# Six pairs of input-projection column tiles by Strassen's seven products

## The chip, the cores and the metric

The kernel runs on one core of one Trainium2 chip. The metric is the device time of one execution, in microseconds (us); a time given for a kernel is the median of its runs. The engines are TensorE (PE), VectorE (DVE), ScalarE (ACT), GpSimd (POOL) and SyncE (SP, which here only issues DMAs).

## The reference

Two layers, each a mixer with a residual and then a cross-attention with a residual; a last RMSNorm. All in float32, sequence 1024, model width 1024. The part that matters here is the mixer's input projection: one matrix product, whose 3200 output columns (25 tiles of 128) feed three groups of heads.

```python
xn = rms_norm(h, norm_mix[l])
proj = xn @ w_in                     # (1024 x 1024) @ (1024 x 3200)
gq, gk, gv, glr, ggate, cc, cb, ch, cgate, cq, ckv, kr, mgate = split(proj)
o_gla  = rms_norm(gla_chunked(gq, gk, gv, log_a(glr)), gla_norm) * silu(ggate)
o_conv = cb * causal_conv3(cc * ch, conv_w) * silu(cgate)
qh, kvh = rms_norm(cq, g) @ w_uq, rms_norm(ckv, g) @ w_ukv
o_mla  = causal_attention(rope(qh), rope(kvh, kr)) * silu(mgate)
h = h + concat(o_gla, o_conv, o_mla) @ w_out
```

## The kernel before, in words

**Products.** Activations lie transposed: 128 features on the partitions, 512 positions in a row, so the model width is eight tiles k, and the sequence two halves c. PE multiplies in a reduced type, so each operand is a sum of a high and a low part (`_h`, `_l`), and `mm3` (L298) makes a product of three matmuls: hi·hi (L301), hi·lo (L302), lo·hi (L303), each 128x512.

**The input projection** (`win`, L393). A column tile i of `w_in` is loaded by SP as 128x1024 (`wraw`, L118, two buffers "wr"), ACT casts the high part (L127), and the low part is subtracted in two halves of 128x512 by POOL, or for every fourth tile by DVE (`wsplit`, L123; `sub`, L149). Then for each half c 8 x 3 = 24 matmuls sum into one PSUM bank, and DVE multiplies the bank by R, the reciprocal norm of each position (L402). The gain of the norm is already in the split activations `x1` (`h_x_h`, `h_x_l`). A layer has 25 tiles: 0 to 6 GLA's q, k, v; 7 to 9 its gate `gg`; 10 to 13 and 14 to 17 the convolution's `cc`, `ch`, `cb`, `cg` for two blocks; 18, 19 the latent `cq`; 20, 21 the latent `ckv`; 22 to 24 the attention's gate `mg`. Each gate tile goes through `silu` (L405): three ACT operations, one on DVE, one on ACT, and a product on POOL.

**GLA** has a front (`gla_front`, one chain per pair of heads, over ACT, POOL and DVE), transposes of the values (`v_tokens`, L442: PE transposes `gvt`, ACT copies them out at L453), and a body (`gla_body`, L526) of many small matmuls (`at`, `o`, `up`, `kTps`), whose POOL share is `osq` (128x384).

**What sets the order.** `layers` (L1143 to L1199) takes generators and weaves them: a yield is a piece of work, and `weave` and `chain` say which piece is written when. From that program order a scheduler makes a fixed order of instructions for each engine. Each engine runs its list in order; a semaphore wait holds up all that stands behind it on that engine. Tiles come from pools with a fixed number of buffers (`BUFS`). SP has one list for all DMAs.

In the stretch at stake each layer writes gates and the first convolution block as fill between the pieces of the two GLA bodies, then the two latents (`latent`, L670), each with its own two column tiles, then the second convolution block (`conv`, L626), with the rotary key `krope` and the first keys `mla_k` between, then the attention.

Of the kernel before, what the change touches and what calls it, by code (L numbers as in the profile page):

```python
# [22 lines left out]
KT = D // P  # L23
# [32 lines left out]
def chain(*gens):  # L56
    for g in gens:
        yield from g


def run(g):
    for _ in g:
        pass


BUFS = {"s": 64, "p": 9, "pt": 4, "tq": 1}
# [14 lines left out]
    "wk": (0, 2), "wv": (0, 2), "wq": (0, 2),  # L81
}


class Trunk:
# [344 lines left out]

    def in_q(self, l, p, tags=("mm", "S")):
        self.gq[p] = self.g2(f"gq{l}_{p}")
        yield from self.win(l, 5 * p, f"gq{l}_{p}", lambda c: self.gq[p][c], tags)
# [71 lines left out]
    def gla_start(self, l):  # L505
# [16 lines left out]
        for c in range(2):  # L522
            for dst, (q, r) in enumerate(((0, 64), (1, 0), (1, 0), (0, 64))):
                nc.sync.dma_start(self.kr[c][dst * 16 : dst * 16 + 16], self.gq[q][c][r : r + 16])
# [101 lines left out]
    def conv(self, l, j):  # L626
        nc = self.nc
        base = 10 + 4 * j
        tags = PAIR[f"conv{j}"]
        u = self.g2(f"cc{l}_{j}")  # L630
        y = self.g2(f"cy{l}_{j}")
        self.cy[j] = y
        yield from self.win(l, base, f"cc{l}_{j}", lambda c: u[c], tags)
        tmp = {}

        def dst(name):
            def f(c):
                tmp[c] = self.g(f"{name}{l}_{j}_{c}", tag="pt")
                return tmp[c]
            return f  # L640

        w = [self.gain(l, "conv", 2 * k + j) for k in range(3)]
        c = 0
        for _ in self.win(l, base + 1, f"ch{l}_{j}", dst("ch"), tags):
            self.mul(nc.gpsimd, u[c], u[c], tmp[c])
            nc.scalar.activation(y[c], u[c], AF.Copy, scale=w[2])
            for s in (1, 2):
                nc.vector.scalar_tensor_tensor(
                    y[c][:, s:], u[c][:, : 512 - s], w[2 - s], y[c][:, s:], op0=ALU.mult, op1=ALU.add
                )  # L650
                if c == 1:
                    nc.vector.scalar_tensor_tensor(
                        y[1][:, :s], u[0][:, 512 - s :], w[2 - s], y[1][:, :s], op0=ALU.mult, op1=ALU.add
                    )
            c += 1
            yield
        c = 0
        for _ in self.win(l, base + 3, f"cg{l}_{j}", dst("cg"), tags):
            self.silu(tmp[c], f"cgs{l}_{j}_{c}")
            self.mul(nc.gpsimd, y[c], y[c], tmp[c])  # L660
            c += 1
            yield
        c = 0
        for _ in self.win(l, base + 2, f"cb{l}_{j}", dst("cb"), tags):
            self.mul(nc.gpsimd, y[c], y[c], tmp[c])
            c += 1
            yield


    def latent(self, l, what, base):  # L670

        nc = self.nc
        raw = [self.g2(f"{what}{l}_{i}") for i in range(2)]
        acc = self.g2(f"{what}acc{l}", tag="pt")
        for i in range(2):
            c = 0
            for _ in self.win(l, base + i, f"{what}{l}_{i}", lambda c: raw[i][c], PAIR[f"lat{i}"]):
# [6 lines left out]
                c += 1  # L684
                yield
# [446 lines left out]
    def go(self, out):  # L1132
        tc = self.tc
        self.mgd = [self.dram(f"mgd{i}_", 2, [P, 512]) for i in range(3)]
        self.ggd = [self.dram(f"ggd{i}_", 2, [P, 512]) for i in range(3)]
        self.god = self.dram("god", NT, [P, 384])
# [6 lines left out]
    def layers(self, out):  # L1143
        for l in range(self.depth):
# [11 lines left out]
            run(self.in_q(l, 1, PAIR["q1"]))  # L1156
            if l == 0:
                run(self.mem_prelude())
            run(self.in_k(l, 1, PAIR["k1"]))
            if l == 0:  # L1160
                self.rope_args()
            self.gla_start(l)
            gates = [self.gate(l, 22 + i, self.mgd[i], f"mg{l}_{i}") for i in range(3)]
            values = chain(*(self.in_v(l, f, PAIR["gv"]) for f in (1, 2)), gates[0])
            weave((values, 0.75), (chain(self.gla_front(l, 0), self.gla_front(l, 1)), 1))
            vt = self.v_tokens(l)
            next(vt)
            next(gates[1])
            run(vt)
            fill = chain(  # L1170
                *gates[1:],
                *(self.gate(l, 7 + i, self.ggd[i], f"gg{l}_{i}") for i in range(3)),
                self.conv(l, 0),
            )
            bodies = [self.gla_body(l, 0), self.gla_body(l, 1)]
            for _ in range(4):
                for b in bodies:
                    next(b, None)
                    for _ in range(2):
                        next(fill, None)  # L1180
            for b in bodies:
                run(b)
            run(fill)
# [4 lines left out]
            conv = self.conv(l, 1)  # L1188
            run(self.latent(l, "ckv", 20))
            run(self.latent(l, "cq", 18))  # L1190
            self.wkn = self.mla_w(l, 2)
            for _ in range(2):
                next(conv)
            run(self.krope(l))
            run(self.mla_k(l, 0))
            run(conv)
# [224 lines left out]
```

## Time and profile before

| what | before |
|---|---|
| median of 3 runs (lowest to highest) | 1416.45 us (1416.19 to 1418.07) |
| the profiled execution: its time, its span | 1415.69 us, 1413.9 us |
| PE busy | 1382.9 us (98%) |
| DVE, ACT, POOL busy | 771.0 (55%), 690.0 (49%), 571.7 us (40%) |
| DMA moved | 131.13 MB, 93 GB/s over the span |
| granted TensorE clock over the span | 0.997 |

The span is what the engines' records cover; the execution's time is 1.8 us more. Busy time is the union of an engine's instructions. Matmuls are pipelined, so that the duration of one (0.39 us) is longer than the distance from one to the next.

### The profile page before, as it was taken

To read this page: it belongs to the slowest core of one execution; us is meant where nothing else is said; L and a number is where in the kernel's file an instruction comes from. 1 tells how busy PE (TensorE), PEld (TensorE's weight loads), DVE (VectorE), ACT (ScalarE), POOL (GpSimd) and SP (SyncE) were. 2 spreads that over 40 slices of the span, in tenths; PEclk is the share of its full clock that TensorE was granted. 3 is DMA by queue.
4 is the path that set the end of the run, shared out by engine and by line. 5 is a ranking of instruction groups with operands and counts; after the bars stand their busy time and mean duration, and the time that the engine had idled before them with its cause. 6 is when DMAs were issued, how large, how long until landed. Compare 5 with 4: busy or idle time off the path is not lost.

```text
span 1413.9 us, 19744 instructions
## 1 busy us (share of the span) xinstructions
PE 1382.9 (98%) x7132; PEld 1128.0 (80%) x7132; DVE 771.0 (55%) x1431; ACT 690.0 (49%) x1462; POOL 571.7 (40%) x584
## 2 busy tenths in 40 slices
PE   7998999999999999999999999999999999999998
PEld 6787888888776688888878788888887767888886
DVE  7846445364788554545653632534657883553533
ACT  5446544253777442555431653424557773344543
POOL 6325335215556452353342532441356663414320
PEclk9999999999999999999999999999999999999999
DMA  8131222122122254321522121211232123534403
GB/s 310 53 129 53 77 76 74 47 63 91 45 61 65 92 172 134 121 89 46 185 100 82 49 78 53 89 58 45 83 86 60 33 81 112 194 105 142 156 1 120
DMA packets 61827, 131.13 MB, mean 93 GB/s; under 512 B 7553, under 2 KB 14497, under 8 KB 61729
## 3 DMA queue, kind: packets, MB, share of 16 engines
q1 hardware_dynamic: 61728, 129.87, 28.5%
q8 instruction: 56, 0.92, 0.3%
q14 instruction: 43, 0.34, 0.1%
HBM read 95.76 MB, written 33.55 MB: 91 GB/s over the span
## 4 chain that ended last, share of the span: by engine, by line
PE 83%; DVE 9%; ACT 3%; issue 2%; DMA 2%; POOL 1%; SPq 0%; DVEq 0%; POOLq 0%; ACTq 0%
PE op_ps L301 4%; PE op_ps L302 4%; PE op_ps L303 4%; PE av L848 4%; PE pt L834 3%; PE xqps L301 2%; PE xqps L302 2%; PE xqps L303 2%; PE s L301 2%; PE gg_ps L301 2%; PE gg_ps L303 2%; PE gg_ps L302 2%; PE s L303 1%; PE s L302 1%; DVE gla_a L479 1%
## 5 line engine op out<-in xcount | busy, mean ns | idle before, releaser
L149 POOL TENSOR_TENSOR win_l<-win_r,win_h 128x512 fp32r<-128x512 f32 x76 | 104.1, 1391 | 196.4 <-ACT win_h L127 191.6
L805 POOL TENSOR_SCALAR p<-p,sm 128x128 f32<-128x128 f32 (+3 forms) x144 | 87.8, 619 | 63.8 <-DVE sm L803 41.5
L127 ACT CAST win_h<-win_r 128x1024 fp32r<-128x1024 f32 x50 | 52.4, 1049 | 123.5 <-PE gg_ps L302 36.6
L303 PE MATMUL op_ps<-mix_h,wout_l 128*128 128x512 f32 x256 | 99.9, 390 | 0.0
L302 PE MATMUL op_ps<-mix_l,wout_h 128*128 128x512 f32 x256 | 99.8, 390 | 0.0
L301 PE MATMUL op_ps<-mix_h,wout_h 128*128 128x512 f32 x256 | 99.0, 393 | 0.0
L799 ACT ACTIVATE p<-s,nm 128x128 f32<-128x128 f32 (+3 forms) x144 | 83.2, 581 | 27.1 <-DVE nm L795 13.8
L791 DVE TENSOR_REDUCE nm<-s 128x1 f32<-128x128 f32 (+3 forms) x144 | 78.4, 551 | 3.1 <-PE s L303 1.1
L834 PE MATMUL pt<-ident,p 128*128 128x128 f32 x432 | 70.6, 280 | 1.6 <-POOL p L805 1.5
L834 PEld LDWEIGHTS pt<-ident,p 128*128 128x128 f32 x432 | 49.7, 140 | 27.3 <-issue 13.7
L848 PE MATMUL av<-ph,V 128*64 128x256 f32 x480 | 69.6, 375 | 0.0
L149 POOL TENSOR_TENSOR wout_l<-wout_r,wout_h 128x512 fp32r<-128x512 f32 x32 | 43.3, 1376 | 42.5 <-ACT wout_h L127 34.4
L301 PE MATMUL s<-k_h,q_h 128*128 128x128 f32 (+3 forms) x144 | 55.2, 386 | 1.3 <-ACT p L799 0.6
L301 PEld LDWEIGHTS op_ps<-mix_h,wout_h 128*128 128x128 f32 x256 | 47.7, 188 | 10.5 <-issue 0.8
L302 PEld LDWEIGHTS op_ps<-mix_l,wout_h 128*128 128x128 f32 x256 | 48.1, 188 | 9.9
L303 PEld LDWEIGHTS op_ps<-mix_h,wout_l 128*128 128x128 f32 x256 | 48.1, 188 | 9.8
L842 ACT COPY ph<-pt 128x512 f32<-128x512 f32 (+1 forms) x72 | 39.6, 549 | 23.7 <-PE pt L834 20.6
L301 PE MATMUL xqps<-op_x_h,wq_h 128*128 128x512 f32 x128 | 51.1, 399 | 0.0
L1005 POOL TENSOR_SCALAR xp<-xp,xsm 128x256 f32<-128x256 f32 x64 | 29.8, 482 | 51.4 <-DVE xsm L1003 51.3
L303 PE MATMUL xqps<-op_x_h,wq_l 128*128 128x512 f32 x128 | 50.4, 393 | 0.0
L302 PE MATMUL xqps<-op_x_l,wq_h 128*128 128x512 f32 x128 | 50.2, 392 | 0.0
L302 PE MATMUL s<-k_l,q_h 128*128 128x128 f32 (+3 forms) x144 | 49.9, 347 | 0.0
(502 smaller groups left out, 4292.5 us busy)
## 6 DMA issues: line engine op xcount, KB each, us to landing
win_r<-in_w_in SPq DMA_DIRECT2D x50, 512.0 KB, 3.6
wout_r<-in_w_out SPq DMA_DIRECT2D x16, 512.0 KB, 4.0
x<-in_x SPq DMA_DIRECT2D x16, 256.0 KB, 6.3
hd<-h SPq DMA_DIRECT2D x16, 256.0 KB, 4.0
op0r<-hd SPq DMA_DIRECT2D x16, 256.0 KB, 4.0
hd<-op0r SPq DMA_DIRECT2D x16, 256.0 KB, 2.9
wq_r<-in_w_mem SPq DMA_DIRECT2D x8, 512.0 KB, 3.8
wk_r<-in_w_mem SPq DMA_DIRECT2D x8, 512.0 KB, 3.6
```

Of the source, the lines that this page charges most:

```text
L127: ins = self.nc.scalar.copy(hi, raw)
L149: eng.tensor_tensor(lo, src, hi.bitcast(F32), op=ALU.subtract)
L301: nc.tensor.matmul(ps, a[0], b[0], start=first, stop=False, **k)
L302: nc.tensor.matmul(ps, a[0], b[1], start=False, stop=False, **k)
L303: nc.tensor.matmul(ps, a[1], b[0], start=False, stop=last, **k)
L791: nc.vector.tensor_reduce(nm[:, b : b + 1], ps[:, :w], axis=AX.X, op=ALU.max, negate=True)
L799: nc.scalar.activation(x[:, :w], ps[:, :w], AF.Exp, bias=nm[:, 0:1], accum_out=sm[:, b : b + 1])
L805: nc.gpsimd.tensor_scalar(pr[b][:, :w], pr[b][:, :w], sm[:, 0:1], 1.0, op0=ALU.mult, op1=ALU.mult)
L834: nc.tensor.transpose(ps[:, o : o + P], prob[qi][kt // 4][:, (kt % 4) * P : (kt % 4 + 1) * P], self.ident,)
L842: nc.scalar.copy(pt[:, :w], ps[:, :w])
L848: nc.tensor.matmul(av[own if j == 0 else other, q0:256], self.V[kt][:, 64 * h : 64 * h + 64], pt[:, j * 256 : j * 256 + 256 - q0], start=( ...
L1005: nc.gpsimd.tensor_scalar(pr[:, j], pr[:, j], sm[:, j : j + 1], 1.0, op0=ALU.mult, op1=ALU.mult)
```

## The change

Per layer 12 of the 25 column tiles are taken in six pairs, `PAIRS` = (20, 21), (18, 19), (10, 11), (13, 12), (14, 15), (17, 16). For a pair, the product is a 2 x 2 block product: the halves of the model width (k 0 to 3, k 4 to 7) by the two tiles on one side, the two halves of the sequence on the other. It is computed with seven block products of 4 x 3 = 12 matmuls (Winograd's form) in place of eight. For this:

- `a_side` loads the layer's input `hd` again (16 loads of 128x512), ACT puts the gain on (16), POOL multiplies by R (16) and makes the four sums of the activations (16), SP stores them (16, `sd`). `s_parts` loads the sums back (16), ACT casts the high parts, and DVE (k 0, 2) or POOL (k 1, 3) subtracts the low ones.
- `w_first` makes, per pair, the split weights of the first tile (`wsplit`), two sums of the second by the first in place (two POOL subtractions of 128x512), a further sum `t4` on DVE, its cast on ACT and its low part on DVE, and stores the sums (512 KB, `wtd`). `w_second`, twice per pair, loads 768 KB or 512 KB of weights and sums, makes a further sum the first time (POOL or DVE), casts on ACT, and subtracts low parts, half on POOL, half on DVE.
- `wave1` runs three block products per pair and stores two of them (`pd`), `wave2` two and stores two partial sums (`ud`), `wave3` the last two. DVE takes each out of PSUM, with R or with a stored sum, and POOL adds once. The results go to sinks, from which `conv` and `latent` take them; their own projections are gone.
- In `layers` value tile 1 stands before the memory prelude, the first GLA front is written among values and q, the transposes of the values stand before the second front, and `rope_args` (layer 0) after it. The gates still fill the first pieces of the GLA bodies, with `a_side` beside them, and wave 1 and `s_parts` come after the gates. Waves 2 and 3 run for the latents' pairs first, and for the four pairs of the convolution in and after the latents.
- "wr" has 4 buffers in place of 2, "s" 60 in place of 64.

```diff
-BUFS = {"s": 64, "p": 9, "pt": 4, "tq": 1}
+BUFS = {"s": 60, "p": 9, "pt": 4, "tq": 1}
+PAIRS = ((20, 21), (18, 19), (10, 11), (13, 12), (14, 15), (17, 16))
-        raw = self.wp.tile(shape, F32, tag="wr", bufs=2, name=name + "_r")
+        raw = self.wp.tile(shape, F32, tag="wr", bufs=4, name=name + "_r")
+    def a_side(self, l):
+        for k in range(4):
+            t = {}
+            for m, c in ((k, 1), (k + 4, 1), (k, 0), (k + 4, 0)):
+                x = self.g(f"sa{l}_{m}_{c}")
+                nc.sync.dma_start(x, self.hd[m][c])
+                nc.scalar.activation(x, x, AF.Copy, scale=self.gain(l, "mix", m))
+                self.mul(nc.gpsimd, x, x, self.R[c])
+                t[(m // 4, c)] = x
+            a11, a12, a21, a22 = t[(0, 0)], t[(1, 0)], t[(0, 1)], t[(1, 1)]
+            nc.gpsimd.tensor_tensor(a22, a21, a22, op=ALU.add)
+            nc.gpsimd.tensor_tensor(a21, a11, a21, op=ALU.subtract)
+            nc.gpsimd.tensor_tensor(a11, a22, a11, op=ALU.subtract)
+            nc.gpsimd.tensor_tensor(a12, a12, a11, op=ALU.subtract)
+            for j, x in enumerate((a22, a11, a21, a12)):
+                nc.sync.dma_start(self.sd[j][k], x)
+            yield
+    def w_first(self, l, n):
...
+        r1, r2 = raws
+        hi, lo = self.wsplit(r1, sh, f"win{l}_{i1}")
+        nc.gpsimd.tensor_tensor(r2[:, :4], r2[:, :4], r1[:, :4], op=ALU.subtract)
+        nc.gpsimd.tensor_tensor(r2[:, 4:], r2[:, 4:], r2[:, :4], op=ALU.subtract)
+        t4 = self.g(f"t4_{l}_{n}", tag="tq", shape=[P, 4, P])
+        nc.vector.tensor_tensor(t4, r1[:, 4:], r2[:, 4:], op=ALU.subtract)
+        nc.sync.dma_start(self.wtd[n], r2)
+        nc.scalar.copy(w4[:, :4], t4)
+        self.sub(nc.vector, w4[:, 4:], t4, w4[:, :4])
...
+    def w_second(self, l, n, j):
...
+        if j == 0:
+            nc.sync.dma_start(r, src)
+            (nc.vector if n % 2 else nc.gpsimd).tensor_tensor(r[:, 4:], r[:, 4:], r[:, :4], op=ALU.subtract)
+            nc.sync.dma_start(r[:, :4], self.wtd[n][:, 4:])
+        else:
+            nc.sync.dma_start(r[:, :4], self.wtd[n][:, :4])
+            nc.sync.dma_start(r[:, 4:], src[:, 4:])
+        nc.scalar.copy(hi, r)
+        for h, e in ((0, nc.gpsimd), (4, nc.vector)):
+            self.sub(e, lo[:, h : h + 4], r[:, h : h + 4], hi[:, h : h + 4])
...
+    def wave2(self, l, pairs):
...
+        for n in pairs:
+            if n != pairs[-1]:
+                head(n + 1)
+                yield
+            p4 = self.spilled(l, f"q4_{l}_{n}", self.pd[n][1])
+            self.prod(x[n], w[n][1], s3, False)
+            u = self.g(f"u3_{l}_{n}", tag="pt")
+            nc.vector.tensor_tensor(u, x[n], p1[n], op=ALU.add)
+            nc.sync.dma_start(self.ud[n][1], u)
+            k = self.sink[PAIRS[n][0]]
+            nc.gpsimd.tensor_tensor(k.tile(1), u, p4, op=ALU.add)
+    def wave3(self, l, pairs):
...
+            u3 = self.spilled(l, f"v3_{l}_{n}", self.ud[n][1])
+            self.prod(y[n], w[n][0], s1, True)
+            k = self.sink[PAIRS[n][1]]
+            nc.vector.tensor_tensor(k.tile(1), y[n], u3, op=ALU.add)
...
     def layers(self, out):
...
+            sides = self.a_side(l)
+            first = self.wave1(l)
+            parts = chain(self.s_parts(l, 1), self.s_parts(l, 2))
+            for i in range(7):
+                next(bodies[(i + 1) % 2], None)
+                next(sides, None)
+                if i > 2:
+                    next(parts, None)
+                    next(parts, None)
+                for _ in range(2):
+                    if next(fill, 0) == 0:
+                        next(first, None)
+                        next(first, None)
...
+            weave((self.wave2(l, (0, 1)), 1), (chain(self.s_parts(l, 0), self.s_parts(l, 3)), 2))
+            run(self.wave3(l, (0, 1)))
+            rest = self.wave2(l, (2, 3, 4, 5))
```

Counted over the two layers, PE has 4364 matmuls of 128x512 in place of 4508, POOL 420 two-input operations of 128x512 in place of 286, DVE 472 in place of 378, SP 734 DMAs in place of 466 (244 more of 256 KB and 24 more of 512 KB).

Three places of the order, layer 0. **POOL, up to the weights of tile 17.** Before, this is the step from the latents to the second convolution block (`_l` tiles are low parts that PE reads):

```order
L149 TENSOR_TENSOR win_18_l<-win_18_r,win_18_h 128x512 x2
L149 TENSOR_TENSOR wlat_2_l<-wlat_2_r,wlat_2_h 128x384 x2
L149 TENSOR_TENSOR win_14_l<-win_14_r,win_14_h 128x512 x2
L149 TENSOR_TENSOR win_17_l<-win_17_r,win_17_h 128x512 x2
L152 TENSOR_TENSOR cc_1_0_2546<-cc_1_0_2546,ch_1_0_2703 128x512
```

In the change it is the end of wave 1 (`win_16_r` and the like are weight sums, `sl` low parts of activation sums, `w2r` a sum for wave 2):

```order
L519 TENSOR_TENSOR win_12_r<-win_12_r 128x512
L518 TENSOR_TENSOR win_15_r<-win_15_r,win_14_r 128x512
L183 TENSOR_TENSOR win_13_l<-win_13_r,win_13_h 128x512 x2
L183 TENSOR_TENSOR sl_2_1_2160<-sr_2_1_2157,sh_2_1_2159 128x512
L519 TENSOR_TENSOR win_15_r<-win_15_r 128x512
L518 TENSOR_TENSOR win_16_r<-win_16_r,win_17_r 128x512
L519 TENSOR_TENSOR win_16_r<-win_16_r 128x512
L183 TENSOR_TENSOR win_14_l<-win_14_r,win_14_h 128x512 x2
L183 TENSOR_TENSOR sl_2_3_2303<-sr_2_3_2300,sh_2_3_2302 128x512
L186 TENSOR_TENSOR osq_1_7_2284<-osb_1_6_2262 128x384
L537 TENSOR_TENSOR w2r_0_0_2513<-w2r_0_0_2513 128x512
L183 TENSOR_TENSOR win_17_l<-win_17_r,win_17_h 128x512 x2
```

What stood nearly alone among waits for ACT is now the tail of a list of POOL work that begins with `a_side`.

**PE, at the first use of tile 17's low part.** Before:

```order
L706 MATMUL yps_1_2622<-krp_1_2623,dup 128x512
L301 MATMUL cg_1_ps_2749<-h_x_h_197,win_17_h 128x512
L302 MATMUL cg_1_ps_2749<-h_x_l_198,win_17_h 128x512
L303 MATMUL cg_1_ps_2749<-h_x_h_197,win_17_l 128x512
L301 MATMUL cg_1_ps_2749<-h_x_h_210,win_17_h 128x512
```

and in the change (`wx_5`, `wy_5` are the banks of the last pair in wave 1):

```order
L337 MATMUL wy_4_2392<-h_x_h_457,w_0_4_2351 128x512
L335 MATMUL wx_5_2454<-h_x_h_247,win_17_h 128x512
L336 MATMUL wx_5_2454<-h_x_l_248,win_17_h 128x512
L335 MATMUL wy_5_2455<-h_x_h_433,w_0_5_2422 128x512
L336 MATMUL wy_5_2455<-h_x_l_434,w_0_5_2422 128x512
L337 MATMUL wx_5_2454<-h_x_h_247,win_17_l 128x512
L335 MATMUL wx_5_2454<-h_x_h_260,win_17_h 128x512
```

It comes over 300 rows earlier on PE (row 1018 in place of row 1325), right behind the GLA bodies and the gates.

**SP, behind the rotary key.** Before, the key's two halves are stored (`yd`) and read back (`k`), with weight loads among them:

```order
L712 DMA yd_0_92<-yh_0_2615 128x512
L712 DMA yd_0_94<-yl_0_2616 128x512
L120 DMA wlat_0_r<-in_w_lat 128x768
L751 DMA k_0_h_2633<-yd_0_92 64x512
L751 DMA k_1_h_2637<-yd_0_92 64x512
```

In the change the partial sums of the last two pairs (`ud`, from DVE) are stored behind the key's stores, and the sum `v_0_4` is read back from what was just stored:

```order
L920 DMA yd_1_143<-yh_1_3010 128x512
L920 DMA yd_1_145<-yl_1_3011 128x512
L608 DMA ud_1_125<-u_0_4_3030 128x512
L608 DMA ud_1_127<-u_0_5_3049 128x512
L580 DMA v_0_4_3137<-ud_1_125 128x512
L580 DMA v_0_3_3176<-ud_0_122 128x512
L874 DMA cgl_0_0_3204<-cgd_0_84 128x512
```

A round trip through memory that had no counterpart now stands in SP's list between wave 2 and wave 3.

## Rows read from the trace of the kernel before

**Rows 1.** The page, its first part: busy time and share of each engine.

```profile
PE 1382.9 (98%) x7132; PEld 1128.0 (80%) x7132; DVE 771.0 (55%) x1431; ACT 690.0 (49%) x1462; POOL 571.7 (40%) x584
```

**Rows 2.** The page, chain of work that ended last: shares by engine.

```profile
PE 83%; DVE 9%; ACT 3%; issue 2%; DMA 2%; POOL 1%; SPq 0%; DVEq 0%; POOLq 0%; ACTq 0%
```

**Rows 3.** PE's waits: engine, line, for whom: us in total, times, longest.

```profile
PE gvt L449 <- ACT gv L453: 7.1, 3, 4.5
```

**Rows 4.** Timeline of PE: start, us, line, tiles, count, idle before and releaser.

```profile
127.42 1.28 PE L449 MATMUL gvt<-ident,vf 128*128 128x128 f32 x6 [4.46 <-ACT gv L453]
...
128.93 0.63 PE L302 MATMUL mg_ps<-h_x_l,win_h 128*128 128x512 f32 x1
129.35 0.63 PE L303 MATMUL mg_ps<-h_x_h,win_l 128*128 128x512 f32 x1
```

**Rows 5.** Timeline of PE in the stretch of the GLA bodies.

```profile
205.79 0.39 PE L303 MATMUL ch_ps<-h_x_h,win_l 128*128 128x512 f32 x1
...
215.11 0.39 PE L302 MATMUL ch_ps<-h_x_l,win_h 128*128 128x512 f32 x1
...
216.25 0.60 PE L545 MATMUL at<-gq,gk 128*128 128x128 f32 x4
216.69 0.49 PE L569 MATMUL up<-gv,kT 128*128 128x192 f32 x2
217.01 0.61 PE L545 MATMUL at<-gq,gk 128*128 128x128 f32 x4
...
219.31 0.35 PE L558 MATMUL o<-gv,atb 128*128 128x96 f32 x2
...
220.11 0.48 PE L303 MATMUL ch_ps<-h_x_h,win_l 128*128 128x512 f32 x1
```

**Rows 6.** Windows: stretch, length, busy of PE, PEld, DVE, ACT, POOL, PEclk, DMA share, GB/s.

```profile
13.00:40.00 27.00, 26.20 (x125) 21.24 (x125) 25.66 (x28) 15.63 (x27) 23.45 (x16) 1.00 0.79 284
...
129.00:135.00 6.00, 6.00 (x28) 4.99 (x27) 0.69 (x1) 2.74 (x6) 2.11 (x2) 0.82 0.37 142
99.00:345.00 246.00, 240.81 (x1170) 202.52 (x1169) 119.62 (x183) 112.62 (x207) 93.45 (x78) 0.99 0.20 65
```

**Rows 7.** Window 0 to 13 us, same columns.

```profile
0.00:13.00 13.00, 5.92 (x19) 3.27 (x19) 5.75 (x12) 4.41 (x6) 2.76 (x8) 1.00 0.78 252
```

**Rows 8.** Groups of POOL between 99 and 345 us, by shape: busy, mean ns, idle before.

```profile
L152 POOL TENSOR_TENSOR osq<-osb 128x384 f32<-128x384 f32 x8 | 6.6, 826 | 10.7 <-ACT osb L579 10.7
...
L152 POOL TENSOR_TENSOR cy<-cy,cg 128x512 f32<-128x512 f32 x4 | 5.2, 1291 | 0.3
```

**Rows 9.** Groups of DVE between 99 and 345 us, by shape.

```profile
L149 DVE TENSOR_TENSOR win_l<-win_r,win_h 128x512 fp32r<-128x512 f32 x8 | 5.4, 720 | 0.5 <-ACT win_h L127 0.3
```

**Rows 10.** Timelines of POOL and of DVE, 26 to 32 us.

```profile
26.19 4.70 POOL L292 TENSOR_TENSOR h_acc<-h_acc,h_sq 128x512 f32<-128x512 f32 x3
...
26.23 1.80 DVE L163 SCALAR_TENSOR_TENSOR h_x_l<-h,gains,h_x_h 128x512 fp32r<-128x512 f32 x1
27.95 0.68 DVE L351 COPY h<-xt 128x512 f32<-128x512 f32 x1
28.56 1.18 DVE L163 SCALAR_TENSOR_TENSOR h_x_l<-h,gains,h_x_h 128x512 fp32r<-128x512 f32 x1
...
30.26 1.17 DVE L163 SCALAR_TENSOR_TENSOR h_x_l<-h,gains,h_x_h 128x512 fp32r<-128x512 f32 x1
```

**Rows 11.** Timelines of DVE and POOL, the gate tile's second half.

```profile
153.56 0.69 DVE L402 TENSOR_TENSOR mg<-mg_ps,h_acc 128x512 f32<-128x512 f32 x1 [0.46 <-PE mg_ps L303]
...
158.73 1.29 POOL L152 TENSOR_TENSOR mg<-mg,mg_2s 128x512 f32<-128x512 f32 x1
```

**Rows 12.** DMA issues: queue, count, KB each, median us from issue to landing.

```profile
op0r<-hd SPq DMA_DIRECT2D x16, 256.0 KB, 4.0
...
mgd<-mg SPq DMA_DIRECT2D x12, 256.0 KB, 2.0
```

**Rows 13.** The page, costliest groups: busy, mean ns of one, idle before.

```profile
L127 ACT CAST win_h<-win_r 128x1024 fp32r<-128x1024 f32 x50 | 52.4, 1049 | 123.5 <-PE gg_ps L302 36.6
```

More of the change, by code (lines that the diff above doesn't have):

```diff
@@ new lines, in s_parts, with prod @@
+    def s_parts(self, l, j):
+        nc = self.nc
+        self.Sp[j] = []
+        for k in range(4):
+            raw = self.g(f"sr{l}_{j}_{k}", tag="pt")
+            nc.sync.dma_start(raw, self.sd[j][k])
+            hi, lo = self.g(f"sh{l}_{j}_{k}", F32R), self.g(f"sl{l}_{j}_{k}", F32R)
+            self.split(hi, lo, raw, eng=self.pick("sp", k))
+            self.Sp[j].append((hi, lo))
+            yield
+    def prod(self, ps, w, xs, first):
+        for k, x in enumerate(xs):
+            self.mm3(ps, w(k), x, first and k == 0, k == len(xs) - 1, skip_group_check=True)
@@ new lines, in wave3, with head @@
+    def wave3(self, l, pairs):
+        nc = self.nc
+        s1, s4 = self.Sp[0], self.Sp[3]
+        w, y = {}, {}
+        def head(n):
+            w[n] = self.w_second(l, n, 1)
+            y[n] = self.psum(("S", "mm", "S", "t")[n % 4], f"vy{l}_{n}")
+            u3 = self.spilled(l, f"v3_{l}_{n}", self.ud[n][1])
+            self.prod(y[n], w[n][0], s1, True)
+            k = self.sink[PAIRS[n][1]]
+            nc.vector.tensor_tensor(k.tile(1), y[n], u3, op=ALU.add)
+        head(pairs[0])
+        yield
+        for n in pairs:
+            if n != pairs[-1]:
+                head(n + 1)
+                yield
+            u2 = self.spilled(l, f"v2_{l}_{n}", self.ud[n][0])
+            self.prod(y[n], w[n][1], s4, False)
+            k = self.sink[PAIRS[n][1]]
+            nc.vector.tensor_tensor(k.tile(0), y[n], u2, op=ALU.add)
+            k.done(0)
+            k.done(1)
+            yield
+            if n in self.after:
+                yield from self.after[n]
@@ L431, in in_q, with sinks @@
+    def sinks(self, l):
+        self.sink = {}
+        for j in range(2):
+            self.sink[13 + 4 * j] = GateSink(self, self.cgd[j], f"cg{l}_{j}")
+            for i in range(3):
+                self.sink[10 + 4 * j + i] = Sink(self, f"c{i}{l}_{j}")
+        for i in range(18, 22):
+            self.sink[i] = Sink(self, f"lat{l}_{i}")
     def in_q(self, l, p, tags=("mm", "S")):
@@ L672, in latent @@
         nc = self.nc
[L673 to L674 removed]
+        raw = [self.sink[base + i].t for i in range(2)]
+        acc = self.g2(f"{what}acc{l}", tag="p")
         for i in range(2):
[L676 to L677 removed]
+            for c in range(2):
                 if i == 0:
@@ L1155, in layers @@
             weave(*((g, 1) for g in head))
-            run(self.in_q(l, 1, PAIR["q1"]))
+            run(self.in_v(l, 1, PAIR["gv"]))
             if l == 0:
                 run(self.mem_prelude())
-            run(self.in_k(l, 1, PAIR["k1"]))
+            self.gla_start(l)
+            fill = chain(self.in_v(l, 2, PAIR["gv"]), self.in_q(l, 1, PAIR["q1"]))
+            weave((fill, 1), (self.gla_front(l, 0), 1))
+            for c in range(2):
+                self.kr_rows(l, c, 1)
+            vt = self.v_tokens(l)
@@ new lines, in layers @@
+            k1 = self.in_k(l, 1, PAIR["k1"])
+            next(vt)
+            next(k1)
+            run(vt)
+            run(k1)
+            gates = [self.gate(l, 22 + i, self.mgd[i], f"mg{l}_{i}") for i in range(3)]
+            gates += [self.gate(l, 7 + i, self.ggd[i], f"gg{l}_{i}") for i in range(3)]
+            bodies = [self.gla_body(l, 0), self.gla_body(l, 1)]
+            fill = chain(*gates)
+            front = self.gla_front(l, 1)
+            for i in range(4):
+                next(front)
+                next(fill)
+                if i == 1:
+                    next(bodies[0])
@@ L1160, in layers @@
+            run(front)
             if l == 0:
                 self.rope_args()
[L1162 to L1180, printed above, removed]
+            self.sinks(l)
+            self.Sp = [None] * 4
+            sides = self.a_side(l)
[11 more added lines that the diff above has]
+                        next(first, None)
@@ L1181, in layers @@
             for b in bodies:
                 run(b)
-            run(fill)
+            run(sides)
+            weave((first, 1), (parts, 1))
             if l == 0:
```

158 lines of the change are left out of this document (119 added, 39 removed).

## The prediction, made before the kernel ran

> **What bounds the kernel now.** I first read the shares of the engines [rows 1]: PE is busy 98% of the span, the next engine, DVE, 55%, POOL 40%. The chain of work that ended last says the same of the path: 83% of it is PE [rows 2]. So time taken from PE is time of the kernel, as long as no other engine is made late for it, and what has to be read is the room that the others have in the one stretch that the change rewrites. That is 99 to 345 us in layer 0, and its twin in layer 1. There PE is busy 240.8 of 246 us, DVE 119.6, ACT 112.6, POOL 93.5, and the DMA engines 20% [rows 6]. Averages leave room for much; the order of the lists decides.
>
> The price of one matmul of 128x512 is not its 0.39 us, which overlaps its neighbours. From the start at 205.79 to the start at 215.11 us there are 41 steps [rows 5], so 9.32 / 41 = 0.227 us each.
>
> **What the change removes.** PE loses 144 matmuls: 144 x 0.227 = **-32.7 us**. Nothing hides this part, since PE is on the path wherever they stood.
>
> A second gain is a by-product. PE waits 7.1 us for ACT's copies of the transposed values, 4.5 of them at once [rows 3], and the matmuls behind that wait stand 0.42 us apart at first [rows 4]; over 129 to 135 us the granted clock is 0.82 [rows 6], so the first part of it ran at the lower of the clock's two levels, after an idle PE. In the changed list of ACT the copies stand before the second GLA front instead of behind it, with 44 matmuls (10 us) on PE between the first front's last step and the first transposes. The bounds are 0 and 7.1 us plus 0.18 x 6 = 1.1 us of slow clock; since the first front's chain is still ahead, I take a little over half: **-5 us**.
>
> **What it adds on POOL.** 134 operations of 128x512, half per layer, at 1.29 us [rows 8]: 67 x 1.29 = 86 us on top of 93.5 in a stretch that becomes some 230 us long. On average they fit. But they stand in one run. From the product of the last `mg` half to the low part of tile 17 (first place of the order) I count 59 operations of 128x512 and 7 of 128x384: 59 x 1.29 + 7 x 0.83 = 81.9 us. The run can't start before that half's silu is ready for POOL, 158.73 - 153.56 = 5.2 us after DVE begins to take it out of PSUM [rows 11]. So POOL's list needs 87.1 us. PE comes to that low part after 316 matmuls (71.7 us) and 98 small GLA matmuls: each float32 matmul has two records there, so two `at` take 216.69 - 216.25 = 0.44 us, one `up` 0.32, four `o` 220.11 - 219.31 = 0.80 [rows 5]. With 34 at 0.22 (`at` and `kTps`), 12 at 0.32 and 52 at 0.20, that is 21.7 us, 93.4 in all. POOL would be 6.3 us early if nothing disturbed it.
>
> Two things do. The first is DVE. POOL's three sums at 26.19 us took 4.70 us instead of 3.87 while DVE ran three operations with two operands from SBUF, and these took 1.80, 1.18 and 1.17 us [rows 10] against 0.72 for one that has less company [rows 9]; the copy out of PSUM between them kept its 0.68. So such a DVE operation costs POOL 0.83 / 3 = 0.28 us there. In the run DVE has 23 of full size and 14 of 128x192: 23 x 0.28 + 14 x 0.105 = 7.9 us, so that POOL is 1.6 us late. The second is POOL's own gaps: its products wait for ACT and for loads through SP. In its densest stretch before, POOL was idle 3.55 of 27 us [rows 6], which over this run would be 12; none is the other bound. Its work here has mostly been loaded earlier, so I take 3. PE thus stands some 5 us in wave 1 of each layer (bounds 0 and 13.6): **+10 us**. What is late next is the transfer list: SP's load of the half weight for wave 2 waits for POOL's sum `w2r_0_0`, and everything behind it on SP waits too.
>
> The Trainium skill has a harsher rule for this ("SBUF — State Buffer", section "Who interferes with whom"): a DVE operation with two SBUF inputs and a GpSimd operation that reads SBUF exclude each other, and the loser is blocked for the whole instruction. Here [rows 10] speak against the full price, as POOL lost 0.83 us and not the three operations' whole time, but for the mechanism, as the PSUM copy was untouched. What it would make of the sum is the first rival.
>
> **What it adds elsewhere.** DVE gets 47 operations per layer, 47 x 0.72 = 34 us, and in layer 0 the angles of the rotary embedding (17 operations, 12 us by the same row [rows 9]), on 119.6: 166 of about 230 us. ACT gets 44 operations, at the price of its longest cast [rows 13] 46 us, on 112.6. Neither becomes a bound; the angles stand among the gates' evacuations, where a full PSUM bank can hold up PE: bounds 0 and 5 us, **+2 us** once.
>
> DMA: per layer 38 MB more. Waves 1 to 3 with the activation sums move about 36 MB in the 504 matmuls of the waves (114 us) and 13 us of other PE work between them: 285 GB/s. The densest stretch before had 284 GB/s at a share of 0.79 [rows 6], so the rate can be had, with a fifth to spare, but not with the waits of [rows 7], 252 GB/s. Where a spilled sum is needed again there is a round trip of 2.0 us for the store and 4.0 for the load [rows 12], and SP runs its list in order. The worst place is the third one of the order: the last pairs' sums stand behind the rotary key's stores. Between that key's matmuls and the need of the sum PE has 72 matmuls, 16 us; ACT's and DVE's steps (four of 0.7), the round trip and two issues come to 10. Bounds 0 and 6 us, since a blocked DVE or SP uses up the spare; I take 2.5 per layer for all such trips: **+5 us**.
>
> Last, a stop of PE is followed by matmuls at the lower clock: behind the one of 4.46 us the six us at 0.82 lose 1.1 us [rows 4, 6]. For one or two such stops I take 1.5 per layer: **+3 us** (bounds 0 and 5).
>
> **The sum**, against the profiled execution of 1415.7 us (0.8 under the median of 1416.45, within the runs' own spread): 1415.7 - 32.7 - 5 + 10 + 2 + 5 + 3 = **1398 us**.
>
> **The rivals.**
>
> *A, slower: DVE and POOL exclude each other.* Then each of the 23 operations takes 0.72 us from POOL's run and each of the small ones 0.27: 20.4 us instead of 7.9. POOL is 87.1 + 20.4 - 93.4 = 14.1 us late, with the 3 us of gaps 17.1 per layer instead of 5: 1398 + 2 x 12.1 = **1422 us**. It decides from about 14 us of lateness per layer (gain gone). For it: DVE operations stretched to 1.80 us, as if they waited for a POOL operation's end. Against it: POOL's small loss in the same rows. The rule of the Trainium skill named above describes this case. Chance 0.18.
>
> *B, slower: the transfers set the pace of the waves.* At the 252 GB/s of the first 13 us [rows 7], 36 MB take 143 us where PE needs 127: 16 us per layer, in which POOL's 5 are hidden, and SP's order adds its round trips. 1398 + 2 x 11 = **1420 us** to 1430 with longer trips. For it: wave 2 alone asks 1.8 MB per 24 matmuls (5.45 us), 337 GB/s, more than any stretch of before. Against it: its loads are issued ahead, four weight buffers instead of two, and other work lies between. Chance 0.12.
>
> *C, all is hidden.* POOL is early, no trip is waited for, the copies' wait goes: 1415.7 - 32.7 - 7 = **1376 us**. For it: the averages of the stretch. Against it: POOL's run has 6 us of room in 93. Chance 0.09.
>
> **How the numbers follow.** The forecast's case has 0.61 (its own range 1384 to 1414: POOL's stop from 0 to 12 us per layer and the small terms at their bounds). What a measurement of this kernel can tell from no change is about 0.2%, 2.8 us. Faster than that: C, nearly all of the forecast's case and a little of A and B, 0.64. Within it: 0.08, the upper edge of the forecast and the lower of A and B. Slower: the rest of A and B, 0.28. The range for 8 in 10 leaves out most of C below and the tail of A and B above: 1380 to 1428.
>
> **What would show it.** Right: PE has 4364 matmuls of 128x512, its busy time falls by some 30 us; PE's waits name POOL low parts (`win_l`, `sl`) in wave 1 with some 5 us per layer, and the wait for the values' copies is below 4 us; DMA share of 0.7 to 0.8 in the waves. Wrong to A: POOL's operations average over 1.6 us in the stretch, POOL busy 90% from the last `mg` gate to tile 17, PE waits of 15 us per layer there. Wrong to B: PE's waits name DVE or ACT steps whose own wait is a DMA. Wrong to C: no wait over 1 us in the waves. If the time came out above 1430, something that I priced small (order on SP, buffers, clock) would be at work.

## The result, and the profile after

| | before | after |
|---|---|---|
| median of the runs | 1417.26 us (4 runs) | 1505.93 us (4 runs, 1501.25 to 1507.12) |
| profiled span | 1413.9 us | 1505.3 us |

The ratio is 1.062, 95% interval 1.0595 to 1.0644: the change makes the kernel slower by 89 us. The page's first part of the changed kernel, against [rows 1], and its largest DMA queue:

```profile
PE 1388.7 (92%) x6988; PEld 1118.8 (74%) x6988; DVE 892.7 (59%) x1525; ACT 744.9 (49%) x1550; POOL 773.4 (51%) x718
q1 hardware_dynamic: 100320, 206.43, 42.0%
```

PE has its 144 matmuls fewer, and is yet busy for 1388.7 us instead of 1382.9. It stands idle for 1505.3 - 1388.7 = 116.6 us instead of 31.0. So the 91.4 us between the spans are 85.6 us of more idle time and 5.8 of more busy time, and the latter is -32.7 for the matmuls that are gone, at the forecast's price, and so +38.5 for those that remain. Most of the second number is the clock. Its mean granted share is 0.970, before 0.997, so 0.030 x 1505 = 45 us of full speed were not granted, before 4. Laid beside PE's busy time, the clock's records put 30.5 of the 45 us on busy time, before 3.4: the clock has 27 of the 38.5 us. The other 11 were not taken apart.

Where it went, by the first start of the score matmuls (`s`) and of the output projection (`op_ps`) in layer 0 (a tile's instructions: count, min/median/max ns, first to last start), before and after:

```profile
L301 PE MATMUL op_ps<-mix_h,wout_h x256: 389/389/503, 470.3 to 1255.6; 128*128 128x512 f32 x128
L301 PE MATMUL s<-k_h,q_h x144: 221/393/504, 351.6 to 1154.3; 128*128 128x512 f32 x72, 128*128 128x128 f32 x24, 128*128 128x256 f32 x24, 128*128 128x384 f32 x24
```
```profile
L335 PE MATMUL op_ps<-mix_h,wout_h x256: 387/389/504, 519.1 to 1346.9; 128*128 128x512 f32 x128
L335 PE MATMUL s<-k_h,q_h x144: 220/397/583, 393.3 to 1245.5; 128*128 128x512 f32 x72, 128*128 128x128 f32 x24, 128*128 128x256 f32 x24, 128*128 128x384 f32 x24
```

The scores start 41.7 us later where 16.4 us of matmuls are gone, so 58 us were lost ahead of them; from there to the output projection it is 125.8 us instead of 118.7. What comes behind, layer 1 in the main, loses much the same: 1505.3 - 1413.9 - 48.8 = 42.6 us net of its 16.4.

PE's waits in the changed kernel (engine, line, for whom: us in total, times, longest; its first lines, without two; one of them is the wait for the input `x`, 6.7 us in both kernels):

```profile
PE up L796 <- ACT kT L767: 23.4, 2, 15.9
PE yps L914 <- DVE krp L183: 9.7, 4, 3.5
...
PE vx L335 <- DVE u L595: 5.7, 5, 2.1
PE cq_ms L297 <- DVE cq_al L183: 5.6, 4, 1.9
PE o L785 <- ACT osb L806: 4.8, 5, 2.4
PE vy L335 <- ACT sh L193: 4.6, 3, 2.2
...
PE s L335 <- DVE tq L977: 4.4, 3, 2.1
PE s L337 <- DVE q_l L183: 4.0, 2, 2.0
PE qps L335 <- DVE k_l L954: 3.5, 2, 1.8
```

The wait of before, for the values' copies [rows 3], is down to 0.8 us. The waits for DVE's key, norm and first queries and keys (`krp`, `cq_al`, `tq`, `q_l`, `k_l`) are 27 us together; before, the list has in their places only

```profile
PE cq_ms L262 <- ACT cq_ah L159: 0.9, 2, 0.5
...
PE s L301 <- DVE tq L769: 0.5, 2, 0.3
```

No low part of wave 1 is in the whole list: POOL's lateness at tile 17, the largest cost of the prediction, is not waited for by PE at all. The longest wait is one for ACT. Its rows in layer 0, timelines of DVE, ACT, POOL and PE (start, length, line, tiles, idle before and releaser; lines left out are marked):

```profile
149.40 1.68 DVE L446 SCALAR_TENSOR_TENSOR mg_1s<-mg,mg_1s 128x512 f32<-128x512 f32 x1
151.01 1.75 DVE L266 SCALAR_TENSOR_TENSOR ang<-ropen,ang 128x512 f32<-128x512 f32 x1
152.68 1.75 DVE L446 SCALAR_TENSOR_TENSOR mg_2s<-mg,mg_2s 128x512 f32<-128x512 f32 x1
...
154.42 0.68 DVE L266 SCALAR_TENSOR_TENSOR ang<-ropen,ang 128x512 f32<-128x512 f32 x1
...
159.61 0.61 ACT L716 COPY gq<-gq 64x512 f32<-64x512 f32 x1 [2.27 <-DVE gq L715]
160.25 0.59 ACT L767 COPY kT<-kTps 128x512 f32<-128x512 f32 x1
...
150.50 1.71 POOL L519 TENSOR_TENSOR win_r<-win_r 128x512 f32<-128x512 f32 x1
152.16 1.71 POOL L186 TENSOR_TENSOR mg<-mg,mg_1s 128x512 f32<-128x512 f32 x1
155.16 1.40 POOL L186 TENSOR_TENSOR mg<-mg,mg_2s 128x512 f32<-128x512 f32 x1 [1.29 <-ACT mg_2s L447]
...
138.35 0.66 PE L765 MATMUL kTps<-ident,gk 128*128 128x128 f32 x4 [0.34 <-DVE mg L436]
...
160.89 1.01 PE L796 MATMUL up<-gv,kT 128*128 128x192 f32 x2 [15.90 <-ACT kT L767]
```

The copy `kT` is 0.59 us of work on data that PE had ready at 139. It stands in ACT's list behind the second GLA front, whose steps wait for DVE, and DVE takes up to 1.75 us for an operation that takes 0.68 at 154.42, when POOL has nothing to do. This stop is paid twice, as time and as clock. Windows of it and behind it (columns of [rows 6]; the eighth number is the granted clock):

```profile
150.00:160.00 10.00, 0.00 (x0) 0.00 (x0) 9.96 (x11) 3.01 (x6) 6.88 (x5) 0.50 0.74 262
160.00:170.00 10.00, 9.11 (x45) 8.65 (x46) 9.93 (x16) 7.01 (x13) 7.73 (x6) 0.69 0.14 40
```

In waves 2 and 3 the pattern is a chain of loads. Timelines of SP, ACT, DVE and PE:

```profile
290.64 0.38 SPq L498 DMA_DIRECT2D sr<-sd  x1
...
295.62 0.62 ACT L193 CAST sh<-sr 128x512 fp32r<-128x512 f32 x1 [3.02 <-DMA sr<-sd]
...
296.27 0.69 DVE L183 TENSOR_TENSOR sl<-sr,sh 128x512 fp32r<-128x512 f32 x1 [4.33 <-ACT sh L193]
...
297.01 0.51 PE L336 MATMUL vy<-sl,w2h 128*128 128x512 f32 x1 [0.23 <-DVE sl L183]
```

SP issues the load at 290.64, behind its other transfers; it lands 5 us later, ACT casts, DVE subtracts, and PE is released. Followed back in this way through the trace, from releaser to releaser, the chain from 285 us to 100 has 68 us of PE, 49 of DVE, 20 of POOL, 19 of DMA and 12 of ACT; the one from 392 to 285 us has 35 of DMA, 24 of DVE and 17 of PE. Before, PE had 157 of the same 185 us. No engine is full over the whole stage; transfers and three engines in turn are what PE waits for.

### The profile page after: what moved, and what is told of

Its sections match the earlier page's. It is cut to its first block, busy times and chain, and to the rows that moved or that the text cites. A ratio compares the mean times of both kernels' runs of the same rounds, so it can differ in the third digit from the quotient of the medians.

```text
span 1505.3 us, 20504 instructions
## 1 busy us (share of the span) xinstructions
PE 1388.7 (92%) x6988; PEld 1118.8 (74%) x6988; DVE 892.7 (59%) x1525; ACT 744.9 (49%) x1550; POOL 773.4 (51%) x718
## 5 line engine op out<-in xcount | busy, mean ns | idle before, releaser
L183 POOL TENSOR_TENSOR win_l<-win_r,win_h 128x512 fp32r<-128x512 f32 x64 | 91.3, 1447 | 92.9 <-ACT win_h L161 78.9
L161 ACT CAST win_h<-win_r 128x1024 fp32r<-128x1024 f32 x38 | 39.7, 1047 | 83.4 <-PE gv_ps L336 33.7
L337 PE MATMUL s<-k_h,q_l 128*128 128x128 f32 (+3 forms) x144 | 49.7, 352 | 4.0 <-DVE q_l L183 4.0
L183 POOL TENSOR_TENSOR w2l<-w2r,w2h 128x512 fp32r<-128x512 f32 x24 | 35.2, 1467 | 32.9 <-PE vx L337 15.1
L326 POOL TENSOR_TENSOR op_acc<-op_acc,op_sq 128x512 f32<-128x512 f32 x16 | 23.5, 1470 | 52.5 <-ACT op_sq L325 52.5
```

The lines of the kernel that those rows point to most:

```text
L161: ins = self.nc.scalar.copy(hi, raw)
L183: eng.tensor_tensor(lo, src, hi.bitcast(F32), op=ALU.subtract)
L337: nc.tensor.matmul(ps, a[1], b[0], start=False, stop=last, **k)
```

## The experiments

Each time is the median of two executions unless told otherwise, and ratios are to the kernel before, run beside them (1416.2 to 1416.7 us). The question was first which one list costs the time.

**e1, the old order of the first part.** The part of `layers` from the second value tile to the second front is the text of before, `rope_args` included; the loop over the bodies starts with body 0.

```diff
-            weave((fill, 1), (self.gla_front(l, 0), 1))
...
+            weave((values, 0.75), (chain(self.gla_front(l, 0), self.gla_front(l, 1)), 1))
```

> Edit: the part of layers up to the GLA bodies is written as in the kernel before (q, k, prelude, rotary angles, values and first gate woven with both GLA fronts, then the transposes). Theory 'order of ACT's list': ACT's copy of kT stands behind the second front's chain (and, in layer 0, DVE's rotary angles); with the old order the waits of PE for it (15.9 and 7.5 us) go with their slow clock (some 8), and the 7.1 us wait for the values' copies comes back with 2: 1506 - 23 - 8 + 9 = about 1484 us. Theory 'POOL's list' (the activation sums keep POOL full and everything behind waits): the wait only moves on to the bodies, 1500 to 1506. Theory 'transfers': no change, 1503 to 1509.

Measured: 1504.88 us, ratio 1.0625 (1.0558 to 1.0691): no change. The wait for kT fell from 23.4 to 7.2 us, and others took its place:

```profile
PE o L785 <- DVE gg L436: 12.4, 2, 6.4
PE o L785 <- ACT osb L806: 10.9, 2, 6.3
...
PE up L796 <- ACT kT L767: 7.2, 2, 4.0
```

The gates' first matmul (`gg_ps`) of layer 0 comes 17 us earlier, at 150.4 us after 167.8, and wave 2's first (`vx`) only 4 earlier, at 278.4 after 282.5. ACT's order was the place of the wait, not its cause.

**e2, only the rotary angles back.**

```diff
+            if l == 0:
+                self.rope_args()
             self.gla_start(l)
...
             run(front)
-            if l == 0:
-                self.rope_args()
```

> Edit: only the rotary angles (layer 0) go back to their place ahead of gla_start; the rest of the order stays. Theory 'order': layer 0's wait for kT falls from 15.9 us to about layer 1's 7.5, with some slow clock: 1494 to 1498 us. Theories 'POOL's list' and 'transfers': within 3 us of 1506.

Measured: 1514.06 us (1.0659 to 1.0721), 8 us slower than the changed kernel. The longest kT wait came down to 7.7 us, as the first theory had it, and the time did not follow.

**e3, no activation sums on POOL.** Products by R and the four sums are left out.

```diff
-                self.mul(nc.gpsimd, x, x, self.R[c])
...
-            nc.gpsimd.tensor_tensor(a22, a21, a22, op=ALU.add)
...
```

> Leaves out the multiplication by R and the four sums of the activations on POOL (32 operations of 128x512 per layer); loads, gains and stores stay. Theory 'POOL's list': the 13 to 16 us that PE loses in each layer between the kT wait and the end of the GLA bodies go: 1475 to 1482 us. Theory 'order': those waits are ACT's and DVE's own, at most 5 us per layer go: 1496 to 1506. Theory 'transfers': sums are stored earlier, so a few us less in waves 1 and 2, 1498 to 1504.

Measured: 1508.35 us (1.0618 to 1.0680): no change either, though engines were relieved:

```profile
PE 1387.3 (92%) x6988; PEld 1116.4 (74%) x6988; DVE 854.4 (57%) x1525; ACT 742.7 (49%) x1550; POOL 676.0 (45%) x654
```

POOL has 97.4 us less for 64 operations (1.52 each, where I took 1.29), and DVE, which lost no operation, 38.3 us less: 0.60 us of DVE's time for each POOL operation that is gone.

**e4, no spills.** Stores of the spilled products and partial sums and their loads are left out; the additions read R.

```diff
-            nc.sync.dma_start(self.pd[n][0], p1)
...
-        t = self.g(name, tag="p")
-        self.nc.sync.dma_start(t, dram)
-        return t
+        return self.R[0]
```

> Leaves out the stores of the spilled products and partial sums and their loads (48 transfers of 256 KB per layer, 12.6 MB); the additions read a tile that is in SBUF anyway. Theory 'transfers': of the 27 us per layer that PE loses in waves 2 and 3 at least half goes: 1475 us or less. Theory 'order' (the latents' norm and the rotary key stand in DVE's list ahead of what PE waits for): at most 5 us per layer, 1496 to 1506. Theory 'POOL's list': no change in waves 2 and 3.

Measured: 1494.10 us (1.0518 to 1.0579), 12 us less than the changed kernel, between the theories. Followed back from 392 to 285 us, the chain now has some 40 us each of DVE and PE and 12 of DMA: DVE's list was right behind the transfers.

**e5, e1, e3 and e4 together.** The three edits above.

> Three of the earlier edits together: the old front (which alone changed nothing), no sums of the activations on POOL (alone nothing), no spilled products (alone -12 us). Left out: R's multiplication and the four sums, the 48 spill transfers per layer. Theory 'several lists equally late' (PE is released by DVE, POOL, ACT and transfers in turn, and taking one away leaves the next just behind): together far more than the sum of the singles, 1440 to 1470 us. Theory 'one resource not yet touched' (DVE's list, or the weights' transfers): about the sum, 1485 to 1497.

Measured: 1458.95 us (1.0283 to 1.0324). The singles are -1, +2 and -12 us, together -47. This is what lists of nearly equal lateness do: one alone uncovers the next. "One resource not yet touched" falls.

**e11, the sums given back to e5** (e1 and e4 together).

> Old front and no spills, but the activation sums on POOL stay: e5 (1459) with its POOL work given back. Left out: the spill transfers. Theory 'several lists equally late': POOL's 64 operations of 1.29 us cost much here, where transfers no longer hide them: 1480 to 1495 us. Theory 'POOL's sums are hidden' (e3 alone changed nothing): 1459 to 1465.

Measured: 1492.74 us (1.0507 to 1.0569). The same 64 POOL operations that cost nothing in the changed kernel cost 34 us here. In layer 0, 15 of them lie ahead of wave 2 (`vx` starts at 279.9 us instead of 264.5), in the stretch of gates and GLA bodies. There PE waits again for the steps for which it waits in e1:

```profile
PE o L779 <- DVE gg L436: 12.6, 2, 6.8
PE o L779 <- ACT osb L800: 11.0, 2, 5.9
```

POOL reaches PE through them: the chain from 285 us back to 100 has 56 us of POOL and 20 of DVE, in e5 14 and 9.

**e6, the changed order without any Strassen product**, in the kernel before.

```diff
-            run(self.in_q(l, 1, PAIR["q1"]))
+            run(self.in_v(l, 1, PAIR["gv"]))
...
+            for i in range(4):
+                next(front)
+                next(fill)
+                if i == 1:
+                    next(bodies[0])
```

> The kernel before, with the changed order of the first part of a layer (value tile first, rotary angles and second GLA front behind the transposes, first piece of a GLA body inside the second front) and no Strassen product. Theory 'the order alone costs what the kT wait shows' (ACT's list, 23 us of waits and 27 us of slow clock in the changed kernel): 1430 to 1445 us. Theory 'the kT wait comes from the load that Strassen brings on DVE and POOL': 1410 to 1420, with the 7 us for the values' copies gone.

Measured: 1418.82 us (8 runs, ratio 1.0018, 1.0007 to 1.0028). kT is waited for 2.8 us in all, but one wait for DVE (`atb`) takes 7.5. The order alone costs 2 us; the 23 us need the load that Strassen's work puts beside it.

**e7, no activation side.** Old front, no spills, no `a_side`; the parts of the sums are split from a resident tile. All matmuls and all weights' work stay.

```diff
-            raw = self.g(f"sr{l}_{j}_{k}", tag="pt")
-            nc.sync.dma_start(raw, self.sd[j][k])
+            raw = self.R[j % 2]
...
-                next(sides, None)
-            run(sides)
```

> Old front, no a_side at all (no loads, gains, sums and stores of the activations), parts of the sums split from a tile that is resident (no loads), no spills. Left out are the sums of the activations and the spilled products; all 4364 matmuls, the weights' sums, their stores and loads and all evacuations stay. Theory 'several lists equally late': close to what PE needs, 1395 to 1420 us. Theory 'weights' (the sums and second loads of the weights on POOL, DVE and SP bound the waves): over 1450.

Measured: 1438.37 us (1.0138 to 1.0179), above the range of the first theory and below that of the second. With the activations' loads, gains, sums and stores and the spills gone (the split of the sums' parts stays), the seven products still lose 22 us to the eight. PE's first waits:

```profile
PE yps L907 <- DVE krp L183: 13.0, 4, 4.0
...
PE gvt L665 <- ACT gv L669: 6.3, 3, 3.7
PE s L335 <- DVE tq L970: 5.0, 5, 2.1
PE s L337 <- DVE q_l L183: 4.0, 2, 2.0
```

Except for the values' copies, for which the kernel before waits too, PE waits here for DVE, between wave 2 and the attention: for the rotary key and the first queries, which share DVE's list with the norms and the convolution's taps.

**e9, e7 with the key ahead of wave 2.**

```diff
+            run(self.krope(l))
             weave((self.wave2(l, (0, 1)), 1), (chain(self.s_parts(l, 0), self.s_parts(l, 3)), 2))
...
-            run(self.krope(l))
```

> On the kernel without the activations' side and spills (1438 us): the rotary key is made ahead of wave 2 instead of between the latents and the last pairs. Theory 'DVE's tail has no cover' (the latents' norms, the key and the convolution's taps, which stood among projections before, now follow one another with PE waiting): PE's wait for the key, 13 us, goes with its slow clock: 1415 to 1425 us. Theory 'DVE's list is full there, and the wait only changes its name': 1433 to 1438.

Measured: 1469.28 us (1.0328 to 1.0417), 31 us slower than e7. The key's wait fell to 5.7 us; a wait for a sum in wave 3 came that was not there:

```profile
PE vy L335 <- DVE c L619: 16.1, 2, 8.1
```

Neither theory had it that way. In layer 0 PE stands from 323.15 to 331.23 us, and ahead of the sum DVE's list has the latent's norm and its split:

```profile
325.16 3.42 DVE L893 TENSOR_TENSOR lat<-lat,cqacc 128x512 f32<-128x512 f32 x2
328.51 2.06 DVE L197 SCALAR_TENSOR_TENSOR cqp_l<-lat,gains,cqp_h 128x512 fp32r<-128x512 f32 x3
330.50 1.27 DVE L619 TENSOR_TENSOR c<-vy,h_acc 128x512 f32<-128x512 f32 x2
```

In e7 (timeline of DVE) the same steps stand from 313.2 to 319.8 us around the key, and PE's 4.0 us for the key are spent behind the first of them. So the norm was part of that wait, and with the key gone it stands before a sum.

**e10, e9 with the second convolution block woven into the attention.**

```diff
-            run(self.conv(l, 1))
-            run(self.mla(l))
+            weave((self.mla(l), 1), (self.conv(l, 1), 0.2))
```

> The edit of e9, and the second convolution block woven into the attention instead of ahead of it. Theory 'DVE's tail has no cover': the waits of the first attention matmuls for DVE (13 us over both layers) go as well, 1400 to 1415 us. Theory 'full list': 1430 to 1438.

Measured: 1453.93 us (1.0234 to 1.0294): above both ranges, since e9 was, but 15 us below e9.

**e13, the taps alone** (the diff of e10 on e7).

> The kernel of e7 (1438 us: no activation side, no spills, old front) with the second convolution block woven into the attention, the key left where it is. Theory 'the taps are an additive term of DVE's tail': the 15 us between e9 and e10 are had here too: 1420 to 1427 us. Theory 'they counted only because e9 had made the tail later': 1434 to 1438.

Measured: 1430.96 us (1.0077 to 1.0136): -7.4 us, half of what it was worth behind e9 and between the two ranges. The taps without cover are a term, and in this kernel of this size.

**e14, e13 with the other half of the low parts on POOL.**

```diff
-        for h, e in ((0, nc.gpsimd), (4, nc.vector)):
+        for h, e in ((0, nc.gpsimd), (4, nc.gpsimd)):
```

> e13, and the second half of the weights' low parts of waves 2 and 3 (24 operations of 128x512 over both layers) on POOL instead of DVE. Theory 'DVE's list is what PE waits for in waves 2 and 3': 1405 to 1420 us. Theory 'the round trips of the weights' sums through SP are': unchanged or slower by up to 10 us, as POOL's share of the trip gets longer.

Measured: 1435.50 us (1.0109 to 1.0168), 4.5 us slower than e13, though DVE is busy 14 us less (851.8 after 866.1). That is the second theory's range, and the first falls: in this form DVE's busy time is not what PE waits for. That the weights' trip (load, sum, load, cast, low part) is, in its place, is not shown by this alone.

**e12, the complete kernel with both edits of e10.**

> The changed kernel, complete, with the key early and the second convolution block woven into the attention (both edits of e10). Theory 'several lists equally late': transfers and POOL hold the waves anyhow, so less than in e10 is gained: 1485 to 1500 us. Theory 'DVE's tail is a term of its own': the same gain as from e7 to e10.

Measured: 1506.27 us (1.0563 to 1.0704), above the first theory's range: nothing gained.

**e8, the kernel before with its fronts earlier** (three rounds).

```diff
-            weave((values, 0.75), (chain(self.gla_front(l, 0), self.gla_front(l, 1)), 1))
+            weave((values, 0.5), (chain(self.gla_front(l, 0), self.gla_front(l, 1)), 1))
```

> The kernel before with one number changed: values and first gate woven with the two GLA fronts at 0.5 instead of 0.75, so that the fronts are ahead of the values' copies in ACT's list by more matmuls. By the waits of the kernel before (7.1 us for the values' copies, 6.8 us of slow clock behind them): 1407 to 1414 us if the wait goes; 1415 to 1418 if ACT's chain only moves with it.

Measured: 1411.80 us (7 runs, 1411.44 to 1412.82) against 1416.54 us, ratio 0.997 (0.9959 to 0.9981). It beats both kernels. PE's wait for the values' copies, 7.1 us [rows 3], is

```profile
PE gvt L449 <- ACT gv L453: 1.9, 1, 1.9
```

## Why the prediction was wrong

**Right:** 144 matmuls gone (their -32.7 us were not measured by themselves); the wait for the values' copies down to 0.8 us; POOL's work up to tile 17. From the product of the last `mg` half at 170.65 us to the end of tile 17's low part at 274.48 POOL is busy for 89.8 us, and the forecast has 81.9 + 7.9.

**"PE thus stands some 5 us in wave 1 of each layer"** failed. PE never waited at tile 17. Both sides came late there, POOL's half of the low part and PE's need of it:

```profile
271.49 2.99 POOL L183 TENSOR_TENSOR win_l<-win_r,win_h 128x512 fp32r<-128x512 f32 x2 [1.78 <-PE wx L336]
...
275.26 0.39 PE L337 MATMUL wx<-h_x_h,win_l 128*128 128x512 f32 x1
```

POOL had 14 us of gaps in its run instead of 3, the last of them a wait for PE itself. PE came 114 us after the last `mg` half left PSUM (161.31), not 93.4; the window of this stretch has 10.9 us without PE and a clock of 0.93:

```profile
161.31:275.42 114.11, 103.17 (x505) 87.64 (x505) 76.61 (x97) 57.96 (x112) 97.44 (x71) 0.93 0.61 198
```

I compared POOL's list with PE's at one point only, the end, as if PE would run up to it undisturbed. But POOL's run also holds `osq`, the gates' products and the activations' sums, and behind these stand DVE's and ACT's steps of the GLA bodies; PE was stopped there, a few microseconds at a time. That POOL was in time at tile 17 is luck, then. e11 against e5 shows what the sums cost over the two layers where nothing else hides it: 34 us, where the term had 10.

**"Neither becomes a bound"** failed for DVE, and with it "+2": from 150 to 160 us, while PE waits for `kT`, DVE is busy for 9.96 of 10 us. I took from [rows 10] only what DVE costs POOL (0.28 us) and left out what stands in the same rows, that POOL costs DVE more: 1.80 for 0.72. By the forecast's price 94 more DVE operations are 68 us; DVE's busy time rose by 121.7. The rotary angles and the second front were priced as work, not as what stands ahead of other work in a list: `kT`, 15.9 us.

**"+5 us" for the round trips** was too small: without the spills alone it is 12 us, and in the chain of waves 2 and 3 transfers have 35 of 107 us in layer 0. The rate was to be had, with PE never idle from 980 to 1000 us at 302 GB/s:

```profile
980.00:1000.00 20.00, 20.00 (x101) 16.93 (x100) 14.32 (x21) 6.83 (x14) 14.59 (x11) 1.00 0.92 302
```

So rival B's price, the rate, falls, though its sign is there: PE's waits name steps whose own wait is a DMA, as at 295.62. What PE waits for is the length of single trips in SP's one list. Rival A falls short of its own signs: between 170.65 and 274.48 POOL is busy for 87% of the time, an operation of 128x512 takes 1.43 us in the mean, where A's signs were 90% and over 1.6 us, and PE does not wait at tile 17.

**"+3 us" for the clock** was an order too small: 27 us more were not granted while PE was busy. I priced one or two stops of PE in a layer; the nine groups shown of the changed kernel's wait list have 2 + 4 + 5 + 4 + 5 + 3 + 3 + 2 + 2 = 30.

**What the sum lacked** is that the terms are not independent. e1 to e4 show it: each undoes a cost that the trace names, and returns 12 us at most; three together return 47. A sum of waits, each worked out as if all else were on time, has no term for the next list. One reservation: each edit also makes the scheduler order all lists anew, and e2 and e9, which only move work, came out 8 and 31 us slower, so the size of any single one holds this too.

**The cover** was not in it at all: the norms, the taps and the key stood among projections of 24 matmuls; the waves take these away, and DVE's same work stands before an idle PE (the 27 us of waits for it above). The second convolution block's taps are worth 7.4 us (e13).

What is left open: e13 is still some 15 us above the kernel before and about 48 above 1415.7 - 32.7 = 1383. Its clock (0.991) and the key's 13 us are part of that; e9 and e14, which were to move the rest, made it worse, and the rest was not taken apart further. Of the 108 us between the forecast and the time, e7 takes away 68 and the taps 7; 33 stay without a test. Nor were the buffers tested, which the prediction names last: POOL's wait for PE at 271.49, and one of 5.48 us at 236.40, both ahead of a low part, may be waits for a free weight buffer.

## What to carry to other kernels

When an engine is 98% busy, the others may have been fitted around it, as here, and work taken from it uncovers them: price a saving on the bound engine by what its work was covering, list by list, at every place where the bound engine is released, and not only at the end of the longest list. A wait that the trace names is a place, not a cause; test it by taking away two or three suspects together, since one alone may return nothing. The cheapest gain was in the old kernel's own longest wait: one weaving rate, 4.7 us.

## What the runs showed of the hardware

- DVE and POOL side by side, both with two operands from SBUF: 1.68 to 1.75 us for DVE's 0.69, and 1.71 for POOL's 1.29, in step. A pair so takes about 1.7 us, less than 0.69 + 1.29 = 1.98. The Trainium skill ("SBUF — State Buffer", "Who interferes with whom") calls the ports that these two share an exclusive lock and says that the loser is blocked for the whole instruction. That DVE loses some 1.0 us, most of POOL's operation, agrees; that POOL loses 0.42 us, less than DVE's whole operation, does not. Over the kernel, each POOL operation that e3 leaves out gave 1.52 us of POOL and 0.60 of DVE back.
- A short stop can be enough for the lower clock: behind one of 2.09 us at 308.58 the matmuls come to stand 0.42 us apart, and 310 to 320 us have a granted clock of 0.85. It isn't always so: 290 to 310 us, with PE busy for 14.73 of 20 us, have 0.99. PE's timeline at 308:

```profile
308.58 0.50 PE L335 MATMUL vy<-sh,w2h 128*128 128x512 f32 x1 [2.09 <-DVE u L607]
...
309.71 0.63 PE L336 MATMUL vy<-sl,w2h 128*128 128x512 f32 x1
310.13 0.63 PE L337 MATMUL vy<-sh,w2l 128*128 128x512 f32 x1
```

The window of these microseconds:

```profile
310.00:320.00 10.00, 10.00 (x37) 7.27 (x37) 5.61 (x7) 6.33 (x10) 3.55 (x3) 0.85 0.78 262
```

- Stores of 256 KB land in a median of 3.5 to 4.2 us in the stretches that the change fills with transfers, where the gates' stores of before, in stretches with few, have 2.0 [rows 12] (queue, count, KB, median us to landing).

```profile
sd<-sa SPq DMA_DIRECT2D x32, 256.0 KB, 3.5
...
pd<-p SPq DMA_DIRECT2D x24, 256.0 KB, 4.2
```
